# A Fourier front laid out anew: a root per tile in the tables, odd sums inside the eight-row products, four blocks at once

## Chip, cores and metric

The kernel runs on one core of a Trainium2 chip. The metric is the device time of one execution in microseconds (us). TensorE (PE in the profile, PEld for its weight loads), VectorE (DVE), ScalarE (ACT), GpSimd (POOL) and SyncE (SP) each work through a queue of their own in order and wait for each other on semaphores.

## The reference

```python
def fourier_mix(h, w_out):
    hg = h.astype(jnp.float32).reshape(B, S, N_FGROUPS, F_GROUP)      # 512 tokens, 8 groups of 128 features
    f = jnp.fft.fft2(hg, axes=(1, 3), norm="ortho").real
    return f.reshape(B, S, D_MODEL) @ w_out                           # 1024 x 1024

for i in range(2):
    if i == 0:
        x = x + fourier_mix(rms_norm(x, fourier_norm[0]), fourier_w_out[0])
    else:
        x = x + gqa_attention(rms_norm(x, attn_norm[0]), ...)
    x = x + sq_relu_mlp(rms_norm(x, mlp_norm[i]), mlp_w_up[i], mlp_w_down[i])
return rms_norm(x, final_norm)
```

It is done for two sequences of 512 tokens (`x_prompt`, `x_sample`), in float32. The change touches the Fourier layer alone, with which the kernel begins.

## The kernel before

**Numbers.** Most products are float32 accuracy out of three products of rounded parts (`mm3`: high x high, high x low, low x high). `split` makes the parts: ScalarE casts the high half, VectorE subtracts it for the low half. The first sequence's transform runs instead on unrounded float32 operands (`exact_*`), one product of which is two records in the trace.

**Front of a sequence.** The transform of real data is folded. Four tiles `xa[q, t]` of 128 tokens by 1024 features come in; `Front(q, c)` takes tiles 2c and 2c+1: `squares` (ScalarE, sums of squares), `gain` (VectorE, times the norm's gain), `plus` and `minus` (VectorE, sum and difference of the two feature halves; `plus_there` does the sum by an accumulating DMA issued on POOL), `chain` (the six small steps of 1/sqrt), then scaling by the root, and for c = 1 `combine`, which joins the two tiles. `ny` holds a few columns of the difference that need products of their own, with 40 columns of weights (`exact_nyq`, `seq_nyq`). The second sequence's parts are also split (`split_even`, `split_odd`, `split_hi`, `split_lo`).

**Transform.** `transform(q)` multiplies along the tokens for four feature blocks j: cosine into a PSUM tile `ps`, sine into another, over the parts k; then along the features (`feat_stage`: the u and v products, a correction by `feat_nyq` from `an`, and a product that picks odd features' sums into `en`), and splits u and v. Blocks 0 to 2 go together, block 3 after the first feature stage.

**Output weights.** `Fold(j)` loads two halves of the output weights; `minus` makes their difference on VectorE (odd weights) and starts an accumulating DMA on POOL for their sum (even weights). `odd`, `even_hi` and `even_lo` split them. The first sequence then has eight odd products (`odd_outs`, all at once) and eight even ones (`even_outs`, one after the other, in `even(fo)`); `odd_put` and `even_put` take them out of PSUM. An even output has 13 products: three for each of four blocks, and one with the extra rows of `FoldNyq`.

**Order and buffers.** Within `tc.manual_schedule` each engine's queue is in the order of the code, so where a step stands in the code is where it waits. PSUM has eight tiles, `ps()`, handed out in turn. The eight odd outputs hold all of them; even output fo takes the one that `odd_put(fo)` has emptied, and the second transform takes, for its first product and its three pairs of blocks, those that `even_put` 0 to 6 have emptied. `even_put` is a VectorE addition of 510 columns (L726) and a ScalarE copy of two columns (L727) behind it:

```python
nc.vector.tensor_add(both[:, :, 1:], o[:, 1:256].unsqueeze(1).broadcast_to([P, 2, 255]), both[:, :, 1:])
nc.scalar.copy(x[:, 0:257:256], o[:, 0:257:256])
```

The four tables of the second transform (`table(k)`: `dcos`, `dsin`, `dalt`, `dfeat`) and the additions of the input (`add_input`) are DMAs issued on POOL, in the same queue as the memset of `ny` in `combine`. At the start `idle` puts filler products on TensorE until the first data is there.

Of the kernel before, what the change touches and what calls it, by code (L numbers as in the profile page):

```python
# [44 lines left out]
def trunk_kernel(ctx, tc, x_in, xt_in, y_out, tables, rope, gfour, gcol, grow, gfin,  # L45
# [296 lines left out]
    def begin():  # L342
# [5 lines left out]
        for t in range(2, 4):  # L348
            load_x(0, t)
        exact_table(5)  # L350
        exact_table(6)
# [39 lines left out]
    def eights(x):  # L391
        return x[:, 0:512:64].unsqueeze(1).broadcast_to([P, 5, 8])

    class Front:


        def __init__(self, q, c):
            self.q, self.c = q, c
            self.ss, self.r = small(2), small(2)
            self.steps = rsqrt_steps(self.r[:, :2], self.ss[:, :2], 2, 1.0 / D)  # L400
            self.xg, self.p, self.m = [None] * 2, [None] * 2, [None] * 2

        def squares(self, i):
            sumsq(xa[self.q, 2 * self.c + i], self.ss[:, i : i + 1])

# [30 lines left out]
        def scale_both(self, i):  # L436
            if i == 0:
                self.n = sm.tile([P, 2, 5, 8], F32, tag="ny", name=nm("ny"), bufs=2, padded_shape=[P, 2, 8, 8])
            for out, x in ((self.p[i], self.p[i]), (self.n[:, i], eights(self.m[i])), (self.m[i], self.m[i])):
                nc.scalar.activation(out, x, AF.Copy, scale=self.r[:, i : i + 1])  # L440
            parts.append((self.p[i], self.m[i], self.n[:, i]))

        def combine(self):
            (p1, p2), (m1, m2), r, w = self.p, self.m, self.r, 8
            stt = nc.vector.scalar_tensor_tensor
            if self.q == 0:
                n = sm.tile([P, 5, 8], F32, tag="ny", name=nm("ny"), bufs=2, padded_shape=[P, 16, 8])
                stt(n, eights(m2), r[:, 1:2], eights(m1), ALU.mult, ALU.add)
# [60 lines left out]
    def exact_nyq(k, o):  # L509
        nc.tensor.matmul(o[0:40, :258], parts[k][2].rearrange("p a b -> p (a b)"), cosX[k], start=k == 0, stop=k == 2)  # L510
# [26 lines left out]
    def feat_nyq(u, j, first):  # L537
        nyt = nyqs[0][:, j * P : (j + 1) * P]
        nc.tensor.matmul(u[:, :258], nyt, an, start=first, stop=not first)
        return u  # L540

    def feat_stage(q, j, a, b, an, en, u=None):
        if q == 0:
            nc.tensor.matmul(u[:, :258], ftX[:, :P], a, start=False, stop=True)
        else:
            u = ps()
            mm3(u[:, :258], ft(0)[:, 0:P], ft(1)[:, 0:P], a[:, 0], a[:, 1], True, False)
            feat_nyq(u, j, False)
        v = ps()
        pick = slice(6 - 2 * j, 78 - 2 * j)  # L550
        if q == 0:
            nc.tensor.matmul(v[:, :256], ftX[:, P:], b, start=True, stop=True)
            nc.tensor.matmul(en[0:72, :258], pickX[:, pick], a, start=j == 0, stop=j == 3)
        else:
            mm3(v[:, :256], ft(0)[:, P:], ft(1)[:, P:], b[:, 0], b[:, 1], True, True)
            ent = tabs[2][:, 516:594][:, pick]
            nc.tensor.matmul(en[0:72, :258], ent, a[:, 0], start=j == 0, stop=False)
            nc.tensor.matmul(en[0:72, :258], ent, a[:, 1], start=False, stop=j == 3)
# [4 lines left out]

    def nyq_out(q, en):
        t = slot([P, 258], F32R)[0:72]
        nc.scalar.copy(t, en[0:72, :258])
        nc.vector.tensor_sub(t[64:72], en[64:72, :258], f32(t[64:72]))
        un[q] = t
# [4 lines left out]
    def idle(o, n):  # L573

        for _ in range(n):
            nc.tensor.matmul(o[:, :256], filler, filler.unsqueeze(1).broadcast_to([P, 2, P]), start=True, stop=True)  # L576

    def transform(q, mid=lambda: None, hook=lambda at, j: None):
        on, ov = ps(), [(ps(), ps()) for _ in range(3)]
        if q == 0:  # L580
            for k in range(2):
                for j in range(3):
                    exact_even(k, j, ov[j][0])
                exact_nyq(k, on)
                for j in range(3):
                    exact_odd(k, j, ov[j][1])
            mid()
            exact_nyq(2, on)
        else:
            seq_nyq(q, 0, on)  # L590
            for j in range(3):
                seq_part(q, j, 0, *ov[j])
            mid()
            seq_nyq(q, 1, on)
        en = ps()
        nc.scalar.copy(an[0:40], on[0:40, :258])
        nc.vector.tensor_sub(an[32:40], on[32:40, :258], f32(an[32:40]))
        ab = []
        for j in range(3):
            if q == 0:  # L600
                exact_odd(2, j, ov[j][1])
                exact_even(2, j, ov[j][0])
            else:
                seq_part(q, j, 1, *ov[j])
            ab.append(seq_evac(q, *ov[j]))
            hook("seq", j)
        us = [None] * 4
        if q == 0:
            us[0] = feat_nyq(ps(), 0, True)
        feat_stage(q, 0, *ab[0], an, en, us[0])  # L610
        hook("feat", 0)
        o3 = ps(), ps()
        if q == 0:
            for k in range(3):
                exact_even(k, 3, o3[0])
            for k in range(3):
                exact_odd(k, 3, o3[1])
        else:
            for c in range(2):
                seq_part(q, 3, c, *o3)  # L620
# [79 lines left out]
    def even_outs(q, fos):  # L700
        return outs(q, fos, we, 0, 258, (wn.w, un[q]))
# [1419 lines left out]
```

## Time and profile before

| | us |
|---|---|
| three runs | 1671.53, 1672.46, 1674.67 |
| profiled execution, its own time | 1673.12 |
| its span, first to last instruction | 1671.3 |
| TensorE busy | 1661.9 (99%) |
| VectorE busy | 1267.0 (76%) |
| ScalarE busy | 872.1 (52%) |
| POOL busy | 394.3 (24%) |

Times in the trace count from the first instruction. A row of the timeline has start, length, engine, line, operation, what it writes from what it reads, and a count where equal ones are merged; in square brackets is the engine's idle time before it and who ended it. A window's row has, for each engine, busy time and number of instructions. Line numbers are those of the kernel before.

### The profile page before, as it was taken

The page shows a single profiled execution, that of the slowest core. Times are in us where ns is not written, and L with a number is a line of the kernel's source. Part 1 is how long each engine was busy: PE and PEld are TensorE (multiplying, and loading weights), DVE is VectorE, ACT ScalarE, POOL GpSimd, SP SyncE. Part 2 cuts the span into 40 slices and gives each one's busy share as a digit, 9 for nine tenths or more (in the row PEclk, how much of TensorE's full clock was granted, in tenths as well). Part 3 has the DMA queues.
Part 4 walks back from the last instruction along what each step waited for, and adds up shares of the span by engine and source line. Part 5 has one row for each costly group of instructions (what it writes and reads, how often), then busy time and mean ns, then how long its engine had stood idle before and what let it go on. Part 6 is the DMA issues. An engine that isn't in the chain of part 4 may idle for free.

```text
span 1671.3 us, 22288 instructions
## 1 busy us (share of the span) xinstructions
PE 1661.9 (99%) x7843; PEld 1387.8 (83%) x7843; DVE 1267.0 (76%) x1851; ACT 872.1 (52%) x1540; POOL 394.3 (24%) x364
## 2 busy tenths in 40 slices
PE   9999999999999999999999999999999999999998
PEld 8988887888888888888888888888888888888887
DVE  8879776557886869869888877777855487878875
ACT  7766444446342435447688855554454552433334
POOL 3321444221000001325444303004422220000002
PEclk9999999999999999999999999999999999999999
DMA  9843554449775757425501156334544696757532
GB/s 306 257 158 118 204 195 172 151 170 373 250 228 165 248 170 236 168 77 200 166 1 39 64 176 223 117 120 167 211 145 166 221 375 194 233 158 236 178 104 101
DMA packets 122192, 302.48 MB, mean 181 GB/s; under 512 B 12344, under 2 KB 13496, under 8 KB 122080
## 3 DMA queue, kind: packets, MB, share of 16 engines
q1 hardware_dynamic: 98720, 253.53, 43.9%
q0 software_dynamic: 8960, 21.05, 6.0%
q10 hardware_dynamic: 14400, 26.48, 4.2%
q8 instruction: 61, 1.00, 0.2%
q14 instruction: 51, 0.42, 0.1%
HBM read 217.59 MB, written 82.38 MB: 179 GB/s over the span
## 4 chain that ended last, share of the span: by engine, by line
PE 97%; DVE 1%; DMA 0%; ACT 0%; issue 0%; POOL 0%; DVEq 0%; POOLq 0%; ACTq 0%
PE ps L940 74%; PE ps L83 6%; PE ps L81 6%; PE ps L82 6%; PE ps L1535 2%; PE ps L576 0%; PE ps L1514 0%; DMA raw<-w_up 0%; PE ps L191 0%; PE ps L507 0%; PE ps L504 0%; DVE w L87 0%; DVE raw L990 0%; PE ps L199 0%; DVE raw L989 0%
## 5 line engine op out<-in xcount | busy, mean ns | idle before, releaser
L940 PE MATMUL ps<-u,w 128*128 128x512 f32 x4944 | 1130.9, 389 | 1.2 <-DVE t L1018 1.2
L940 PEld LDWEIGHTS ps<-u,w 128*128 128x128 f32 x4944 | 926.6, 188 | 195.9 <-ACT u L973 1.7
L86 ACT CAST w<-raw 128x1024 fp32r<-128x1024 f32 (+1 forms) x216 | 213.7, 994 | 311.5 <-PE ps L940 234.3
L87 DVE TENSOR_TENSOR w<-raw,w 128x1024 fp32r<-128x1024 f32 (+1 forms) x216 | 252.0, 1170 | 75.7 <-ACT w L86 75.4
L86 ACT CAST u<-u 128x1024 fp32r<-128x1024 f32 x144 | 145.0, 1047 | 85.1 <-PE ps L940 36.4
L87 DVE TENSOR_TENSOR u<-u,u 128x1024 fp32r<-128x1024 f32 x144 | 174.3, 1239 | 17.3 <-ACT u L86 16.0
L940 PE MATMUL ps<-u,u 128*128 128x512 f32 x600 | 143.3, 389 | 0.0
L1150 DVE TENSOR_TENSOR u<-ps,u 128x512 f32<-128x512 f32 x160 | 109.9, 688 | 39.8 <-PE ps L940 37.3
L1177 POOL DMA_DIRECT2D raw<-w_sum x32 | 27.7, 865 | 468.2 <-DMA raw<-w_sum 170.8
L1058 POOL TENSOR_TENSOR u<-u 128x512 f32<-128x512 f32 x28 | 37.0, 1321 | 425.9 <-ACT u L955 425.9
L940 PEld LDWEIGHTS ps<-u,u 128*128 128x128 f32 x600 | 112.5, 188 | 24.1 <-ACT u L973 0.4
L81 PE MATMUL ps<-u,u 128*128 128x512 f32 (+2 forms) x340 | 128.7, 380 | 0.0
L83 PE MATMUL ps<-u,u 128*128 128x512 f32 (+2 forms) x340 | 123.7, 365 | 0.0
L82 PE MATMUL ps<-u,u 128*128 128x512 f32 (+2 forms) x340 | 123.6, 365 | 0.0
L182 POOL TENSOR_TENSOR t<-t,t 128x512 f32<-128x512 f32 (+1 forms) x54 | 79.2, 1470 | 187.0 <-ACT t L178 186.1
L954 ACT ACTIVATE t<-t 128x512 f32<-128x512 f32 x64 | 40.5, 632 | 109.2 <-DVE t L1027 95.7
L83 PEld LDWEIGHTS ps<-u,u 128*128 128x128 f32 x340 | 64.2, 189 | 10.5 <-DVE u L87 0.3
L87 DVE TENSOR_TENSOR u<-ps,u 128x512 fp32r<-128x512 f32 (+3 forms) x112 | 68.2, 636 | 5.6 <-ACT u L86 5.0
L82 PEld LDWEIGHTS ps<-u,u 128*128 128x128 f32 x340 | 64.4, 189 | 8.5 <-DVE u L87 0.3
L81 PEld LDWEIGHTS ps<-u,u 128*128 128x128 f32 x340 | 64.4, 189 | 7.8
L1014 DVE TENSOR_TENSOR t<-ps,u 128x512 f32<-128x512 f32 x32 | 22.0, 689 | 59.5 <-PE ps L940 55.8
L86 ACT CAST u<-ps 128x512 fp32r<-128x512 f32 (+3 forms) x112 | 59.5, 557 | 7.7 <-PE ps L1535 6.1
(270 smaller groups left out, 2024.6 us busy)
## 6 DMA issues: line engine op xcount, KB each, us to landing
raw<-w_up SPq DMA_DIRECT2D x80, 512.0 KB, 4.6
u<-spill_t SPq DMA_DIRECT2D x60, 512.0 KB, 6.7
raw<-w_sum SPq DMA_DIRECT2D x56, 512.0 KB, 5.5
u<-spill_b SPq DMA_DIRECT2D x45, 512.0 KB, 6.3
spill_t<-u SPq DMA_DIRECT2D x84, 256.0 KB, 2.0
spill_b<-t ACTq DMA_DIRECT2D x60, 256.0 KB, 4.4
raw<-w_row SPq DMA_DIRECT2D x28, 512.0 KB, 5.0
park<-u SPq DMA_DIRECT2D x24, 512.0 KB, 4.6
```

What stands on the lines that cost most here:

```text
L81: nc.tensor.matmul(out, lh, rh, start=first, stop=False)
L82: nc.tensor.matmul(out, lh, rl, start=False, stop=False)
L83: nc.tensor.matmul(out, ll, rh, start=False, stop=last)
L86: hi = nc.scalar.copy(dst_hi, src)
L87: return hi, eng.tensor_sub(dst_lo, src, f32(dst_hi))
L182: nc.gpsimd.tensor_add(acc[q][:, :n], acc[q][:, :n], s[:, :n])
L940: nc.tensor.matmul(o, w[x][:, sl], h[k][y], start=first and k + i == 0, stop=k == n - 1 and i == 2, skip_group_check=not first)
L954: nc.scalar.activation(t, src, AF.Relu)
L1058: eng.tensor_sub(t[:, 0], b12, b11)
L1150: return nc.vector.tensor_add(x, o, x)
L1177: nc.gpsimd.dma_start(s[:, 1], w[:, 3], accum_op=ALU.add)
L1535: nc.tensor.transpose(pt[:, t * P : (t + 1) * P], probs[t][:, sc * P : (sc + 1) * P], ident)
```

## The change

What it does, in the order of the code:

- The loads: table 1 comes before the fourth tile; table 2 comes behind the first fold's halves; all folds and the second sequence's tiles are asked for earlier in the code.
- The first two tiles get a root each (`apart`), and the root goes into the tables (`table`), not into the tiles; the steps of each root stand between long instructions on VectorE. Filler at the start is 23 products, not 39.
- The odd features' sums are no longer picked by a product for each block. VectorE sums the odd columns of each part (`odd_sums`, `tensor_reduce`), ScalarE copies the sums next to the eight `ny` columns (`put_sums`), and the eight-row products take both, with 56 columns of weights. `put_low` makes the extra rows of the even outputs from their result.
- The first transform is `transform_exact`: four blocks at once in all eight PSUM tiles, nine filler products with zero weights behind the second part, the eight-row products behind the third part, and two feature products ahead of each split.
- `hook0` and what follows are reordered: the differences of folds 0 to 2 in one row on VectorE, all four `even_hi` in one row on ScalarE ahead of the first `odd_put`, the second sequence's `gain`, `minus` and `plus_there` further ahead, the tables on POOL behind even output 1, both `combine`s ahead of the last even outputs.

```diff
-            self.steps = rsqrt_steps(self.r[:, :2], self.ss[:, :2], 2, 1.0 / D)
+            if q == 0 and c == 0:
+                self.apart = [rsqrt_steps(self.r[:, i : i + 1], self.ss[:, i : i + 1], 1, 1.0 / D) for i in range(2)]
+            else:
+                self.steps = rsqrt_steps(self.r[:, :2], self.ss[:, :2], 2, 1.0 / D)
...
+        def table(self, i):
+            t = exact[i][:, :514]
+            nc.scalar.activation(t, t, AF.Copy, scale=self.r[:, i : i + 1])
...
+    def odd_sums(k):
+        s = small(8)
+        x = parts[k][0].rearrange("p (g d i) -> p g d i", g=8, i=2)[:, :, :, 1]
+        nc.vector.tensor_reduce(s, x, AX.X, ALU.add)
+        return s
+
+    def put_sums(k, s):
+        nc.scalar.copy(parts[k][2][:, :, 1:], s.unsqueeze(1).unsqueeze(1).broadcast_to([P, 2, 3, 8]))
...
-        nc.tensor.matmul(o[0:40, :258], parts[k][2].rearrange("p a b -> p (a b)"), cosX[k], start=k == 0, stop=k == 2)
+        nc.tensor.matmul(o[0:56, :258], parts[k][2].rearrange("p a b c -> p (a b c)")[:, :56], cosX[k], start=k == 0, stop=k == 2)
...
+    def put_low(on):
+        norm = 1.0 / math.sqrt(S * P)
+        low = slot([P, 258], F32R)[0:56]
+        nc.scalar.activation(low, on[0:56, :258], AF.Copy, scale=norm)
+        nc.vector.scalar_tensor_tensor(low[32:56], on[32:56, :258], norm, f32(low[32:56]), ALU.mult, ALU.subtract)
+        un[0] = low
...
+    def transform_exact(mid, hook):
+        ov = [(ps(), ps()) for _ in range(4)]
+        for k in range(2):
+            for j in range(4):
+                exact_even(k, j, ov[j][0])
+            for j in range(4):
+                exact_odd(k, j, ov[j][1])
+        idle(ov[3][1], 9, an[:, :P])
+        mid()
+        ab = []
+        for j in range(4):
+            exact_odd(2, j, ov[j][1])
+            exact_even(2, j, ov[j][0])
+            ab.append(seq_evac(0, *ov[j]))
+            hook("seq", j)
+        on = ps()
+        for k in range(3):
+            exact_nyq(k, on)
+        put_an(on)
+        put_low(on)
+        hook("an", 0)
+        o = [feat_exact(*ab[j]) for j in range(2)]
+        for j in range(4):
+            feat_nyq(o[j][0], j)
+            feat_split(0, j, *o[j])
+            hook("feat", j)
+            if 0 < j < 3:
+                o.append(feat_exact(*ab[j + 1]))
...
-    idle(ps(), 39)
+    idle(ps(), 23)
...
+        g0.chain(0, 1)
+        g0.gain(0)
+        g0.chain(2, 3)
+        g0.minus(0)
+        g0.plus_there(0)
+        for j in range(4):
+            fold[j].even_hi()
...
+        odd_put(0, 0, o[0])
...
         even(0)
+        g1.gain(1)
         g1.minus(1)
         g1.plus_there(1)
-        g1.squares(1)
+        for k in range(4):
+            table(k)
         even(1)
+        g0.combine()
+        g1.chain(0, 1)
+        g1.chain(2, 3)
         even(2)
...
-        even(6)
         g1.combine()
         g1.split_hi()
+        even(5)
+        g1.split_lo()
+        even(6)
         even(7)
-        g1.split_lo()
```

The pieces of the queues that the prediction speaks of follow. In them, names like `u_` and `t_` are SBUF tiles, `s_` and `n_` small ones, `ps_` PSUM tiles; numbers differ between the two builds.

VectorE before, from the second sequence's first tile to the four low halves of the even weights (L659; `raw` and the `u_315` tile are the accumulated weights):

```order
L423 TENSOR_TENSOR t_431<-u_429 128x512
L410 TENSOR_TENSOR u_436<-u_321,u_99 128x1024
L423 TENSOR_TENSOR t_438<-u_436 128x512
L141 TENSOR_SCALAR s_259<-s_257 128x2
L143 RECIPROCAL s_260<-s_261 128x2
L144 TENSOR_TENSOR s_262<-s_260 128x2
L145 SCALAR_TENSOR_TENSOR s_262<-s_262,s_259 128x2
L146 SCALAR_TENSOR_TENSOR s_258<-s_262,s_260 128x2
L659 TENSOR_TENSOR w_551<-raw_249,w_551 128x1024
L659 TENSOR_TENSOR w_553<-raw_253,w_553 128x1024
L659 TENSOR_TENSOR w_564<-raw_311,w_564 128x1024
L659 TENSOR_TENSOR w_569<-u_315,w_569 128x1024
```

The same place on VectorE after (L700 are the low halves, L429 `gain`, L442 `minus`):

```order
L141 TENSOR_SCALAR s_160<-s_158 128x2
L429 TENSOR_TENSOR u_545<-u_238,u_99 128x1024
L143 RECIPROCAL s_161<-s_162 128x2
L442 TENSOR_TENSOR t_548<-u_545 128x512
L144 TENSOR_TENSOR s_163<-s_161 128x2
L700 TENSOR_TENSOR w_551<-raw_220,w_551 128x1024
L145 SCALAR_TENSOR_TENSOR s_163<-s_163,s_160 128x2
L700 TENSOR_TENSOR w_553<-raw_226,w_553 128x1024
L146 SCALAR_TENSOR_TENSOR s_159<-s_163,s_161 128x2
L429 TENSOR_TENSOR u_566<-u_240,u_99 128x1024
L700 TENSOR_TENSOR w_555<-raw_230,w_555 128x1024
L700 TENSOR_TENSOR w_557<-u_234,w_557 128x1024
```

The root's steps lie between long instructions now, the second `gain` stands between the second and the third low half, and its `minus` has gone behind the fourth.

VectorE before, at the last even outputs (L726 is `even_put`, L463 to L465 and L87 the second half's `combine`, L479 its low halves):

```order
L726 TENSOR_TENSOR u_443<-ps_697,u_443 128x2x255
L726 TENSOR_TENSOR u_443<-ps_714,u_443 128x2x255
L726 TENSOR_TENSOR u_444<-ps_732,u_444 128x2x255
L463 SCALAR_TENSOR_TENSOR n_153_750<-t_636,s_264,t_606 128x8
L464 SCALAR_TENSOR_TENSOR u_579<-u_612,s_264,u_579 128x512
L465 SCALAR_TENSOR_TENSOR t_636<-t_636,s_264,t_606 128x512
L87 TENSOR_TENSOR ny_748<-n_153_750,ny_748 128x2x8
L726 TENSOR_TENSOR u_444<-ps_760,u_444 128x2x255
L479 TENSOR_TENSOR u_756<-u_579,u_756 128x512
L479 TENSOR_TENSOR u_757<-t_636,u_757 128x512
```

The same place on VectorE after (L769 is `even_put`, L485 to L487 and L87 `combine`, L501 the low halves):

```order
L769 TENSOR_TENSOR u_437<-ps_685,u_437 128x2x255
L769 TENSOR_TENSOR u_438<-ps_703,u_438 128x2x255
L485 SCALAR_TENSOR_TENSOR n_157_721<-t_619,s_165,t_588 128x8
L486 SCALAR_TENSOR_TENSOR u_586<-u_617,s_165,u_586 128x512
L487 SCALAR_TENSOR_TENSOR t_619<-t_619,s_165,t_588 128x512
L87 TENSOR_TENSOR ny_719<-n_157_721,ny_719 128x2x8
L769 TENSOR_TENSOR u_438<-ps_731,u_438 128x2x255
L501 TENSOR_TENSOR u_727<-u_586,u_727 128x512
L501 TENSOR_TENSOR u_728<-t_619,u_728 128x512
L769 TENSOR_TENSOR u_439<-ps_750,u_439 128x2x255
L769 TENSOR_TENSOR u_439<-ps_766,u_439 128x2x255
```

Before, seven `even_put` (0 to 6) stand ahead of the second half's combine and one behind it; now five stand ahead, number 5 behind the combine, and 6 and 7 behind the low halves too.

POOL before, from the second sequence's first root to the first `add_input` (L419 `plus_there`, L430 a masked root for `combine`, L454 the memset of `ny`, L730 `add_input`):

```order
L430 TENSOR_TENSOR s_559<-s_258,mask 128x1
L454 MEMSET ny_585 128x128
L329 DMA u_594<-dcos 128x774
L329 DMA u_596<-dsin 128x1024
L329 DMA u_598<-dalt 128x594
L329 DMA u_600<-dfeat 128x512
L419 DMA u_579<-u_579 128x512
L419 DMA u_612<-u_612 128x512
L730 DMA u_441<-xt 128x1024
```

The same place on POOL after (L438, L449, L476 and L773 are the same steps in that order):

```order
L449 TENSOR_TENSOR s_564<-s_159,mask 128x1
L438 DMA u_566<-u_566 128x512
L438 DMA u_586<-u_586 128x512
L438 DMA u_617<-u_617 128x512
L329 DMA u_622<-dcos 128x774
L329 DMA u_624<-dsin 128x1024
L329 DMA u_626<-dalt 128x594
L329 DMA u_628<-dfeat 128x512
L773 DMA u_436<-xt 128x1024
L476 MEMSET ny_647 128x128
```

The memset of the first `ny`, which ScalarE's cast and VectorE's low half of it wait for, has gone behind all four tables and the first `add_input`, and the tables behind the last two `plus_there`.

More of the change, by code (lines that the diff above doesn't have):

```diff
@@ L741, in trunk_kernel @@
[L741 to L750 removed]
+        g0, g1 = [Front(1, c) for c in range(2)]
+        idle(ps(), 23)
+        f0.squares(0)
+        f0.gain(0, 0, halves_gr[0])
+        f0.root(0, 0, 2)
+        nc.scalar.copy(gr[:, :512], halves_gr[0])
@@ L751, in trunk_kernel @@
+        f0.gain(0, 1, halves_gr[1])
+        nc.scalar.copy(gr[:, 512:], halves_gr[1])
+        f0.root(0, 2, 6)
+        f0.table(0)
+        f0.plus(0)
+        f0.minus(0)
+        f0.squares(1)
+        wn.load()
+        fold = [Fold(0)]
+        exact_table(6)
+        fold += [Fold(j) for j in range(1, 4)]
+        for t in range(NT):
+            load_x(1, t)
+        nc.sync.dma_start(gc, gcol)
+        f0.gain(1)
+        f0.root(1, 0, 3)
         f1.squares(0)
-        f0.scale_both(0)
```

296 lines of the change are left out of this document (133 added, 163 removed).

## The prediction

> **What bounds the kernel now.** I read the page first, then the stages of its first 60 us, then the instructions of each engine there in order of time.
>
> ```profile
> PE 1661.9 (99%) x7843; PEld 1387.8 (83%) x7843; DVE 1267.0 (76%) x1851; ACT 872.1 (52%) x1540; POOL 394.3 (24%) x364
> PE 97%; DVE 1%; DMA 0%; ACT 0%; issue 0%; POOL 0%; DVEq 0%; POOLq 0%; ACTq 0%
> ```
>
> TensorE is the chain that ends last. Behind the Fourier part the change moves nothing, so whatever TensorE gains or loses up to the start of the second sequence's transform goes through to the end. The stages of the front (columns: time, PE, PEld, DVE, ACT, POOL busy, granted clock, DMA share, GB/s):
>
> ```profile
> 10.00:20.00 10.00, 10.00 (x48) 7.11 (x47) 9.79 (x18) 6.71 (x15) 3.71 (x4) 1.00 1.03 409
> 20.00:30.00 10.00, 10.00 (x51) 8.45 (x51) 9.94 (x15) 7.89 (x20) 4.29 (x6) 1.00 1.06 324
> 30.00:40.00 10.00, 10.00 (x86) 10.00 (x85) 9.23 (x15) 8.32 (x13) 4.76 (x7) 1.00 1.06 204
> 40.00:50.00 10.00, 10.00 (x86) 10.00 (x85) 9.42 (x16) 8.85 (x26) 2.42 (x5) 1.00 0.66 181
> 50.00:60.00 10.00, 10.00 (x86) 9.98 (x86) 8.78 (x23) 6.50 (x21) 4.67 (x7) 1.00 0.90 161
> ```
>
> TensorE is full, and VectorE nearly as full: 9.79, 9.94, 9.23, 9.42 and 8.78 of 10 us. There are two bounds side by side here, and a front that is shorter on TensorE alone meets VectorE at once. TensorE's marks (start, length; two records for each float32 product):
>
> ```profile
> 17.86 0.63 PE L510 MATMUL ps<-u,ny 128*40 128x258 f32 x2
> 18.42 0.70 PE L507 MATMUL ps<-u,t 128*128 128x256 f32 x2
> 22.55 1.47 PE L504 MATMUL ps<-u,t 128*128 128x258 f32 x6
> 23.86 1.46 PE L507 MATMUL ps<-u,t 128*128 128x256 f32 x6
> 29.24 0.47 PE L81 MATMUL ps<-u,u 128*128 128x256 f32 x1
> 40.93 0.28 PE L81 MATMUL ps<-u,w 128*128 128x258 f32 x1
> 42.26 0.28 PE L83 MATMUL ps<-u,w 128*128 128x258 f32 x1
> 53.42 0.28 PE L81 MATMUL ps<-u,ny 128*40 128x258 f32 x1
> ```
>
> Six records take 23.86 - 22.55 = 1.31, so a float32 product takes 0.434. Odd output products begin at 29.24, even ones at 40.93 (the fourth fold's low half is first read at 42.26), the second transform at 53.42. From 29 us on TensorE takes one product of 256 columns per 0.12 us (86 in 10 us).
>
> **The change on TensorE up to the odd products.** The filler products:
>
> ```profile
> 1.17 2.93 PE L576 MATMUL ps<-u 128*128 128x256 f32 x12 [1.17 <-DVE mask L369]
> 5.40:7.40 2.00, 1.94 (x9) 2.00 (x10) 1.00 1.01 406
> 7.50:10.90 3.40, 3.40 (x31) 3.40 (x30) 1.00 1.02 403
> ```
>
> The first ten weight loads take 0.20 us each, the later ones 3.40/30 = 0.113, and the last one ends at 10.9. Sixteen fewer end about 1.9 us sooner, near 9.0. Whether table 0 is scaled by then matters little, for the front's end doesn't follow: the third tile pair is VectorE's.
>
> ```profile
> 15.38 0.16 DVE L145 SCALAR_TENSOR_TENSOR s<-s,s 128x2 f32<-128x2 f32 x1
> 15.58 0.16 DVE L146 SCALAR_TENSOR_TENSOR s<-s,s 128x2 f32<-128x2 f32 x1
> 15.65 0.69 DVE L423 TENSOR_TENSOR t<-u 128x512 f32<-128x512 f32 x1
> 17.87 0.74 DVE L450 SCALAR_TENSOR_TENSOR t<-t,s,t 128x512 f32<-128x512 f32 x1
> ```
>
> A root step that the next one waits for costs 0.20, one with an independent instruction behind it 0.07. Ten steps become fifteen, but two thirds of them now stand in front of something independent: 5 x 0.20 + 10 x 0.07 = 1.7, as much as ten cost before. So the combined pair is ready at 17.9 and 18.6, as before, and TensorE, which has done its 16 products at 9.0 + 16 x 0.434 = 16.0 and its nine fillers at 17.1, waits there.
>
> From the pair on, before: 29.24 - 18.42 = 10.8. After: eight products 3.5, three eight-row products, eight feature products 3.5, four short ones 0.5. An eight-row product in the middle of others took 18.42 - 17.86 = 0.56, and some 0.3 of drain ahead of it; three in a row I put at 0.3 + 3 x 0.56 = 2.0 (1.5 if only the first and last pay). Sum 9.5, odd products at 27.6: 1.6 gained (1.2 to 2.1). Some 0.7 of it goes in the odd products' first round, whose seventh and eighth bank wait for the fourth block's splits on VectorE.
>
> **VectorE from 18.5 to the even products.** Now the low halves, `even_lo`, end here:
>
> ```profile
> 31.04 1.23 DVE L87 TENSOR_TENSOR u<-u,u 128x1024 fp32r<-128x1024 f32 x1 [0.56 <-issue]
> 36.64 3.50 DVE L659 TENSOR_TENSOR w<-raw,w 128x1024 fp32r<-128x1024 f32 x3
> 40.28 1.23 DVE L659 TENSOR_TENSOR w<-u,w 128x1024 fp32r<-128x1024 f32 x1 [0.15 <-ACT w L655]
> 18.59 0.37 ACT L596 CAST u<-ps 40x258 fp32r<-40x258 f32 x1 [0.97 <-PE ps L510]
> L1525 DVE TENSOR_REDUCE s<-ps 128x1 f32<-128x512 f32 x64 | 43.7, 684 | 8.9 <-PE ps L83 6.8 <-PE ps L1535 1.9
> ```
>
> The queue ends at 41.5 and TensorE needs it at 42.26: 0.75 of slack. Added: three sums of 256 elements, between 0.16 (the least step) and 0.68 (the row's 512 from PSUM), taken as 0.37 each, 1.1. Added too: VectorE is free at 18.5 + 1.1 + 3 x 1.14 = 23.0, but its next instruction waits for the eight-row products (end 23.6, with ScalarE's 0.37 and a hop 24.1) and then once more for ScalarE's second copy: 1.5 (0.8 to 1.9). Gone: a `minus` moved behind (0.6), root steps between long ones (0.4), the old wait of 0.56 and 0.15 before the last. Two small waits on ScalarE add 0.4. Net +0.9 and the fourth low half at 42.4: that product starts at 42.45 against 42.26. **The gain of 1.6 is gone here and has become a loss of 0.2**; ScalarE's `odd_put`, now behind all four `even_hi`, lets the first even product start at about 40.3 and costs nothing more, if the last accumulated weight lands near 38.6.
>
> **From there to the second transform.** Its seven banks are those that even products 0 to 6 held, in turn, and each comes free with VectorE's and ScalarE's two `even_put` reads. The rows of now:
>
> ```profile
> 43.51 0.75 DVE L465 SCALAR_TENSOR_TENSOR t<-t,s,t 128x512 f32<-128x512 f32 x1
> 45.96 1.22 DVE L410 TENSOR_TENSOR u<-u,u 128x1024 f32<-128x1024 f32 x1
> 48.42 0.68 DVE L423 TENSOR_TENSOR t<-u 128x512 f32<-128x512 f32 x1
> 51.54 1.88 DVE L726 TENSOR_TENSOR u<-ps,u 128x510 f32<-128x510 f32 x3
> 55.16 0.68 DVE L726 TENSOR_TENSOR u<-ps,u 128x510 f32<-128x510 f32 x1
> 56.35 0.69 DVE L479 TENSOR_TENSOR u<-t,u 128x512 fp32r<-128x512 f32 x1
> 45.10 0.72 ACT L489 ACTIVATE t<-u,s 1x512 f32<-1x512 f32 x1
> 38.01 1.70 POOL L329 DMA_DIRECT2D u<-dcos  x1
> 40.81 0.53 POOL L329 DMA_DIRECT2D u<-dfeat  x1
> 49.78 0.89 POOL L419 DMA_DIRECT2D u<-u  x1 [3.54 <-PE ps L697]
> 50.42 2.04 POOL L730 DMA_DIRECT2D u<-xt  x2
> 53.49 0.86 POOL L730 DMA_DIRECT2D u<-xt  x1 [1.03 <-ACT u L727]
> 54.03 0.54 POOL L454 MEMSET ny<- 128x128 f32 x1
> ```
>
> Now puts 0 to 6 are over at 53.42, and only put 7 stands behind the second half's combine. After, VectorE does from 42.4: minus 0.6, gain 1.2, minus 0.6, put 0.6, gain 1.2, minus 0.6 (to 47.3), put 0.6, then the first half's combine (two small, 0.7, 0.75) to 49.5. There it waits for the low half of `ny`, whose high half on ScalarE waits for POOL's memset, and that now stands behind six issues: the last `plus_there` (released at 47.3), four tables and the first `add_input`. Issues follow each other at 0.65 (49.78 to 50.42) and 0.54 (53.49 to 54.03); the four tables took 38.01 to 41.34, 0.83 each, with waits among them. I take 0.65: 47.3 + 5 x 0.65 + 0.54 + 0.54 = 51.7, `ny` at 52.0 (51.4 with 0.54, 53.2 with 0.83). **VectorE stands 2.5 us, with six puts queued behind it.** Then: put 2 to 52.9; behind it ScalarE casts the even half (512 columns, 0.6 to 0.7 by the 45.10 row), so that low half ends at 54.4; ScalarE's one-row repair (0.72) and cast of the odd half, low half at 55.6; the root's last step 55.7; puts 3 and 4 to 56.9, while ScalarE scales the second half's two sums until 57.2; its combine, 2 x 0.7, to 58.6; put 5 to 59.3, two low halves to 60.5, put 6 to 61.1, ScalarE's read to 61.35.
>
> TensorE begins the transform at 42.45 + 0.24 + 7 x 1.56 = 53.6, waits 0.9 for the split halves and puts 3 and 4 until 57.7, for put 5 until 59.6, for put 6 until 61.4. It is past its seventh bank at 61.7; before, 53.42 + 21 x 0.12 = 55.9. **Sum: +5.8.** On VectorE nothing of that can be hidden. What the second half needs later is ready by then.
>
> By the Trainium skill, GPSIMD Engine Reference (Specifications), POOL's SBUF interfaces are shared with VectorE, with contention when a VectorE instruction has two SBUF inputs. The row of 1.70, an issue beside VectorE's low halves with two SBUF inputs, would be such a case; if five of them took that, `ny` would be 5 x 1.05 = 5.2 later and the sum +11. The rows of 0.86 and 0.89, beside VectorE's work too, and the next table's end 41.34 speak against it, so 0.65 stays.
>
> The profiled execution took 1673.12 with a span of 1671.3, and the three runs a median of 1672.46; its rows serve for both. 1672.46 + 5.8 = 1678.3.
>
> **The rivals.**
> (a) *The gain stays.* TensorE's 1.6 us hold if put 6 is done by 54 instead of 61, that is if VectorE loses neither the 1.5 for the eight-row products nor the 2.5 at `ny` and makes 3 us elsewhere. Time 1670.9. For it: TensorE is the page's bound. Against: VectorE's 9.4 of 10. Even with no wait at all TensorE could be at the odd products at 9.0 + 6.9 + 1.1 + 9.5 = 26.5, only 2.7 us sooner. It decides where VectorE's queue reaches put 6 before 55.8. Chance 0.08.
> (b) *POOL does not hold VectorE.* Issues are quicker or their order matters less; VectorE goes on at 49.5. Everything behind is 2.5 to 2.8 us earlier, put 6 at 58.5, since it stands behind both combines anyway: +3.0, 1675.5. Chance 0.18.
> (c) *The waits slow TensorE's clock.* It would work 2.5 us in eight. The opening's fillers were slow from 1.17 to 7.4; if TensorE fell back to 0.20 for as long, 6.2 us would do the work of 3.5: 2.7 more, 1681.0. The Trainium skill, TensorE: Matmul & The Clock Gate (What's actually happening), has the clock fall after an idle window of about 3.4 us, and no wait here is that long; the same page (A second HAM failure mode) has short waits for PSUM banks do it. By the first rule (c) doesn't happen; before's trace has no such waits to show either. Chance 0.12.
>
> **How the numbers follow.** The worked case has 0.56, by itself 1676.3 to 1680.0 (eight-row products -0.7, sums -0.6 to +0.9, issues -0.6 to +1.2, not all at once); 0.06 is left for what I haven't seen, half of it on either side of the faster bound. Eight in ten lie between 1674.0, below (b), and 1681.6, above (c). 0.2% is 3.3 us, about what measurement tells from none: 1675.8 and up counts as slower. That holds (c), the worked case and a third of (b), 0.74; (a), most of (b) and some of the rest are the same, 0.23; for faster TensorE would have to gain over 3.3, more than its front can give: 0.03.
>
> **What would show it.** Right: odd products near 27.6; VectorE idle near 23 to 24 behind the eight-row products and near 49.5 to 52 behind ScalarE's `ny`; TensorE idle in the second transform at each of its last four banks, released by ScalarE's two-column `even_put` copy; the first product of its second half near 61.7. Wrong: no gaps on TensorE there, or the three eight-row products ended before 22.5, or `ny`'s memset before 50.

## The result: 10 us slower, nearly twice what was forecast, and the profile after

The changed kernel takes 1683.64 us (median of six runs, 1683.03 to 1684.87); six runs of the kernel before beside them have 1673.59. The ratio is 1.0062, 95% interval 1.0049 to 1.0075. The forecast was 1678.3 and at most 1681.6: the sign was right, the size not. Medians here and below are of fast runs; two slow ones, 2917.5 us of the second version below and 1838.0 us of the kernel before beside the ninth, are left out.

The page of the changed kernel, busy time and chain that ended last:

```profile
span 1681.5 us, 22269 instructions
PE 1667.6 (99%) x7828; PEld 1388.7 (83%) x7828; DVE 1265.3 (75%) x1858; ACT 870.8 (52%) x1542; POOL 395.7 (24%) x364
PE 94%; DVE 3%; DMA 1%; ACT 1%; issue 1%; POOL 0%; DVEq 0%; POOLq 0%; ACTq 0%
```

The span grew by 10.2 us, and VectorE's share of the chain from 1% to 3%. Stages of the front (columns as before):

```profile
40.00:50.00 10.00, 9.50 (x64) 8.16 (x63) 8.97 (x13) 7.35 (x23) 7.82 (x7) 1.00 0.42 72
50.00:60.00 10.00, 8.46 (x57) 7.09 (x55) 6.09 (x17) 4.91 (x13) 2.82 (x6) 1.00 0.94 219
```

From 40 to 50 us TensorE gets 64 products done where it did 86, though it reads as nearly full and its clock is 1.00. From 50 to 60 VectorE is down to 6.09; 3.57 of what is missing is one wait. TensorE's marks:

```profile
21.71 1.51 PE L532 MATMUL ps<-u,ny 128*56 128x258 f32 x6
23.15 0.70 PE L582 MATMUL ps<-u,u 128*128 128x256 f32 x2
...
27.20 0.28 PE L81 MATMUL ps<-u,u 128*128 128x256 f32 x1
...
41.97 0.38 PE L83 MATMUL ps<-u,w 128*128 128x258 f32 x1 [0.50 <-DVE w L700]
...
56.27 0.31 PE L81 MATMUL ps<-u,ny 128*40 128x258 f32 x1
...
62.45 0.42 PE L521 MATMUL ps<-u,ny 128*40 128x258 f32 x1
...
124.89 0.62 PE L199 MATMUL ps<-ident,s 128*128 128x128 f32 x4 [0.22 <-DVE s L146]
```

Against the kernel before: odd products 2.04 sooner (29.24), fourth low half read 0.29 sooner (42.26), second transform begun 2.85 later (53.42). Its second half, the 22nd product of that transform, is at 62.45, and the last row stands behind the Fourier layers of both sequences. Their rows of before are these:

```profile
55.92 0.28 PE L499 MATMUL ps<-u,ny 128*40 128x258 f32 x1
...
113.90 0.62 PE L199 MATMUL ps<-ident,s 128*128 128x128 f32 x4 [0.23 <-DVE s L146]
```

So TensorE is 6.53 late at the second half and 10.99 late behind the Fourier layers. I call these two places the second half and the layer's end below.

**The first surprise** is in the weight loads of the even outputs (grouped by line and shape; the last figure is idle time before them), from 42 to 56.4 us and then in the second sequence:

```profile
L81 PEld LDWEIGHTS ps<-u,w 128*128 128x128 f32 x28 | 5.3, 190 | 0.9
...
L740 PEld LDWEIGHTS ps<-u,u 56*128 56x128 f32 x8 | 1.5, 183 | 1.1
...
L740 PEld LDWEIGHTS ps<-u,u 48*128 48x128 f32 x8 | 1.5, 183 | 1.1
```

TensorE stands before each of the 16 extra-row products (1.1/8 = 0.14 us) and again behind it. The change cut that product from 72 rows to 56, and to 48 in the second sequence. In time order:

```profile
43.91 0.19 PEld L83 LDWEIGHTS ps<-u,w 128*128 128x128 f32 x1
44.23 0.18 PEld L740 LDWEIGHTS ps<-u,u 56*128 56x128 f32 x1
44.55 0.19 PEld L81 LDWEIGHTS ps<-u,w 128*128 128x128 f32 x1
...
46.50 0.19 PEld L81 LDWEIGHTS ps<-u,w 128*128 128x128 f32 x1
```

The steps into and out of it take 0.32 each where 0.12 is usual, and the even output takes 46.50 - 44.55 = 1.95 instead of 1.56: 0.39 more, 3.1 us per sequence.

**The hold-up** of VectorE behind POOL came as forecast, and longer (rows of POOL, ScalarE, VectorE):

```profile
51.80 0.53 POOL L476 MEMSET ny<- 128x128 f32 x1
...
52.37 0.22 ACT L86 CAST ny<-n 128x32 fp32r<-128x32 f32 x1 [4.74 <-POOL ny L476]
...
52.62 0.19 DVE L87 TENSOR_TENSOR ny<-n,ny 128x32 fp32r<-128x32 f32 x1 [3.57 <-ACT ny L86]
```

**The last banks**: TensorE's weight loads in the second transform, with the idle time ahead of them:

```profile
60.12 0.19 PEld L81 LDWEIGHTS ps<-u,u 128*128 128x128 f32 x1 [1.86 <-ACT u L770]
...
61.91 0.19 PEld L81 LDWEIGHTS ps<-u,u 128*128 128x128 f32 x1 [1.38 <-ACT u L770]
```

Both waits were forecast, for 59.6 and 61.4, with ScalarE's two-column copy as the releaser. The stages behind them:

```profile
62.00:64.00 2.00, 2.00 (x11) 1.86 (x12) 0.26 (x1) 0.39 (x2) 0.89 (x1) 0.56 1.03 152
64.00:66.00 2.00, 2.00 (x12) 2.00 (x12) 0.96 (x3) 1.03 (x4) 0.00 (x0) 0.58 1.13 205
66.00:68.00 2.00, 2.00 (x19) 2.00 (x18) 1.27 (x4) 2.00 (x7) 0.41 (x1) 1.00 1.02 207
```

The clock is 0.56 to 0.58 for some 4 us: 23 products where 38 are usual, 15 x 0.105 = 1.6 us.

### The profile page after: what moved, and what is told of

The parts are those of the page before. It is cut to its first block, busy times and chain, and to the rows that moved or that the text cites. A ratio compares the mean times of both kernels' runs of the same rounds, so it can differ in the third digit from the quotient of the medians.

```text
span 1681.5 us, 22269 instructions
## 1 busy us (share of the span) xinstructions
PE 1667.6 (99%) x7828; PEld 1388.7 (83%) x7828; DVE 1265.3 (75%) x1858; ACT 870.8 (52%) x1542; POOL 395.7 (24%) x364
## 4 chain that ended last, share of the span: by engine, by line
PE 94%; DVE 3%; DMA 1%; ACT 1%; issue 1%; POOL 0%; DVEq 0%; POOLq 0%; ACTq 0%
PE ps L1003 73%; PE ps L81 6%; PE ps L83 6%; PE ps L82 6%; PE ps L1598 2%; DVE u L429 0%; PE ps L1577 0%; PE ps L191 0%; DMA u<-w_four 0%; ACT u L86 0%; DMA raw<-w_sum 0%; DMA u<-spill_t 0%; DVE t L442 0%; DMA u<-x 0%; DVE u L87 0%
## 5 line engine op out<-in xcount | busy, mean ns | idle before, releaser
L87 DVE TENSOR_TENSOR w<-raw,w 128x1024 fp32r<-128x1024 f32 (+1 forms) x216 | 251.2, 1167 | 75.7 <-ACT w L86 75.4
L86 ACT CAST u<-u 128x1024 fp32r<-128x1024 f32 (+1 forms) x140 | 140.7, 1047 | 86.4 <-PE ps L1003 38.9
L87 DVE TENSOR_TENSOR u<-u,u 128x1024 fp32r<-128x1024 f32 (+1 forms) x140 | 168.7, 1232 | 18.3 <-ACT u L86 17.8
L87 DVE TENSOR_TENSOR u<-ps,u 128x512 fp32r<-128x512 f32 (+3 forms) x112 | 68.1, 633 | 6.2 <-ACT u L86 5.7
L1077 DVE TENSOR_TENSOR t<-ps,u 128x512 f32<-128x512 f32 x32 | 22.0, 686 | 60.3 <-PE ps L1003 56.7
```

The lines of the kernel that those rows point to most:

```text
L86: hi = nc.scalar.copy(dst_hi, src)
L87: return hi, eng.tensor_sub(dst_lo, src, f32(dst_hi))
```

## The experiments

The theories: (R) the extra product costs 0.39 us where it has 64 rows or fewer; (H) POOL's queue holds VectorE, and so the banks; (C) the bank waits lower the clock; and whether VectorE's queue as a whole takes the front's gain. The last column is the median less that of the kernel before, run beside it in the same series.

| kernel | second half | layer's end | median | less before |
|---|---|---|---|---|
| before | 55.92 | 113.90 | | |
| changed | 62.45 | 124.89 | 1683.64 | +10.05 |
| 1, 72 rows | 62.68 | 122.01 | 1679.65 | +7.25 |
| 2, clears early | 58.67 | 119.67 | 1677.73 | +5.33 |
| 3, before with 64 rows | 58.88 | 119.86 | 1677.83 | +5.43 |
| 4, products in the waits | 62.54 | 123.53 | 1681.86 | +9.46 |
| 5, both of 1 and 2 | 58.98 | 118.31 | 1676.03 | +3.61 |
| 6, and puts ahead | 56.64 | 115.36 | 1674.14 | +1.72 |
| 7, and VectorE's stands | 56.51 | 115.89 | 1673.91 | +1.49 |
| 8, and one gain late | 56.96 | 116.74 | 1674.54 | +2.01 |
| 9, and tables early | 55.87 | 115.34 | 1673.58 | +1.39 |
| 10, two tables early | 54.80 | 114.81 | 1673.17 | +0.49 |

Differences of medians are to be read with care. The kernel before varies by some 3 us from run to run; its six runs beside the changed kernel have a median of 1673.59, in the other series it is 1672.2 to 1672.7. So a difference between the changed kernel and a version is about 1.2 larger by the medians themselves than by the last column, and differences of 1 us between versions are not clear of the noise. The marks, from one profiled execution each, carry the argument.

**1. The rows back.**

```diff
-        low = slot([P, 258], F32R)[0:56]
-        nc.scalar.activation(low, on[0:56, :258], AF.Copy, scale=norm)
+        low = slot([P, 258], F32R)[0:72]
+        nc.gpsimd.memset(f32(low[64:72]), 0.0)
+        nc.scalar.activation(low[0:64], on[0:64, :258], AF.Copy, scale=norm)
...
-        return outs(q, fos, we, 0, 258, (wn.w[: 48 if q else 56], un[q]))
+        return outs(q, fos, we, 0, 258, (wn.w, un[q]))
```

> The changed kernel with its extra product, the last one of each even output, back to 72 rows (the added rows hold zeros in the weights; the eight-row products take 64 columns and the second sequence's pick 72, so that the rows exist). Rows theory: with 56 or 48 rows TensorE pauses 0.14 us before and 0.13 after that product, and an even output takes 1.95 us instead of 1.56. Then the pauses go, the second transform begins near 53.2 instead of 56.3, but still waits for the same banks until 61.9, so the first eight outputs bring nothing and the second sequence's eight bring 8 x 0.39 = 3.1: 3.1 us faster than the changed kernel (2.6 to 3.6), near 1680.5. If TensorE and not VectorE set the end of the first eight: 6.2 faster. If the pauses come from something else than the count of rows: no change, and the gaps stay.

The layer's end came 2.88 sooner, the median 2.8 by the last column (4.0 by the medians themselves): the second sequence's 3.1 and nothing for the first eight, as expected. The extra product's weight loads in the second sequence (grouped):

```profile
L741 PEld LDWEIGHTS ps<-u,u 72*128 72x128 f32 x8 | 1.5, 191 | 0.0
```

No idle time is left. TensorE where it then stands, in order of time:

```profile
60.07 0.58 PE L81 MATMUL ps<-u,u 128*128 128x258 f32 x1 [1.66 <-ACT u L771]
...
61.87 0.58 PE L81 MATMUL ps<-u,u 128*128 128x256 f32 x1 [0.79 <-ACT u L771]
```

The waits at the banks end where they did (60.12 and 61.91). TensorE, at the transform earlier, has more waits there, and its granted clock is down sooner (0.72 from 58 to 60 us, 0.50 to 64), which fits the second half's 0.23 of delay.

**2. The clears early.** The memset of `ny` is taken out of `combine` and stands in a step of its own, `clear`:

```diff
         o = odd_outs(0, range(KC))
+        g0.clear()
+        g1.clear()
         g0.chain(0, 1)
```

> The changed kernel with the two clears of the second sequence's eight-row tiles put on the Pool queue right behind the odd products, ahead of the accumulating transfers and the four tables. Hold-up theory: VectorE's stand of 3.57 us at 49 to 52.6 goes, puts 2 to 6 come 3.4 us earlier, TensorE's waits for banks (0.14 + 1.86 + 1.38) nearly go, and with them the low granted clock of 62 to 66 us, which costs 1.5: 4.9 us faster than the changed kernel, near 1678.7. If the low clock comes from something else than those waits: 3.4 faster. If VectorE isn't what the banks wait for: no change.

The layer's end came 5.22 sooner, 3.78 of it at the second half and 1.44 behind it, the median 4.7 by the last column. In order of time, the two clears and VectorE's low half of `ny`, which no longer waits:

```profile
33.73 0.68 POOL L467 MEMSET ny<- 128x128 f32 x2
...
48.82 0.18 DVE L87 TENSOR_TENSOR ny<-n,ny 128x32 fp32r<-128x32 f32 x1
```

The stage in which the changed kernel had a clock of 0.56:

```profile
62.00:64.00 2.00, 2.00 (x19) 2.00 (x18) 1.38 (x5) 2.00 (x7) 1.44 (x2) 1.00 1.08 213
```

H holds, and it carries the clock with it. TensorE has no wait in that transform here. It begins it at 56.13, late by its own pauses: in the first sequence the pauses and the hold-up lie side by side, and the longer one counts.

**3. The kernel before with 64 rows.**

```diff
-        return outs(q, fos, we, 0, 258, (wn.w, un[q]))
+        return outs(q, fos, we, 0, 258, (wn.w[:64], un[q][:64]))
```

> The kernel before with its extra product cut from 72 rows to 64 (the last eight, the low part of that operand, are left out of the computation), and nothing else. Rows theory: two pauses of 0.13 to 0.14 us and a slower product at each of 16 even outputs, 0.39 us each, 6.2 us, of which 1.6 go into a later wait of TensorE (1.57 at 260 us) that is there anyway: 4.6 us slower than the kernel before (4 to 6.2), near 1677. If the count of rows isn't the cause: no change within 0.5.

+5.43, ratio 1.0034 (1.0022 to 1.0046), and at the layer's end +5.96, half of it (2.96) by the second half. The row count alone costs this in a kernel that has nothing else of the change (the eight rows of low parts are left out of the computation). Its extra product's weight loads of the first sequence (grouped, idle time last):

```profile
L697 PEld LDWEIGHTS ps<-u,u 64*128 64x128 f32 x8 | 1.5, 183 | 1.1
```

So 64 rows pause like 56 and 48, and 72 do not. What lies between 64 and 72 wasn't tried. By the Trainium skill, TensorEngine Tiling (Array Packing), Key Properties, changing the tiling mode drains TensorE, and its Performance Considerations name row tiling for contractions of 64 rows and fewer. A pause on both sides, 0.14 us before and 0.13 after, and the step between 64 and 72 rows fit that; that the mode changes here no trace shows. The same section has column tiling for 64 weight columns and fewer; there the trace of the changed kernel shows no pause behind such a product with these rounded operands (TensorE in order of time):

```profile
56.54 0.28 PE L83 MATMUL ps<-u,ny 128*40 128x258 f32 x1
56.66 0.28 PE L81 MATMUL ps<-u,u 128*128 128x258 f32 x1
```

From 40 columns to 128 is the usual 0.12.

**4. Products in the waits.**

```diff
             seq_part(q, j, 0, *ov[j])
+            for _ in range((14, 10, 0)[j]):
+                nc.tensor.matmul(ov[0][1][:, :256], zero[:, 0:1].broadcast_to([P, P]), sinT()[:, 0, :256], start=False, stop=False)
```

> The changed kernel with 14 and 10 products with zero weights put into an open bank where TensorE waits 1.86 and 1.38 us for the second transform's last banks, so that it works through those waits. Clock theory: the granted clock of 0.56 to 0.58 from 62 to 66 us comes from the short waits before it, so it stays at 1.00 and 14 products fewer are late: 1.5 us faster than the changed kernel. If the low clock has another cause: it stays, and the time is the same or up to 0.3 worse.

TensorE passes the last bank no sooner:

```profile
62.08 0.39 PE L81 MATMUL ps<-u,u 128*128 128x256 f32 x1 [0.59 <-ACT u L774]
```

But the stage behind it runs at full clock:

```profile
62.00:64.00 2.00, 1.92 (x16) 1.91 (x17) 0.71 (x2) 0.64 (x4) 0.89 (x1) 1.00 1.06 164
```

The layer's end moved by 1.36, the median's distance from the kernel before by 0.6, where the interval (1.0037 to 1.0067) overlaps the changed kernel's: that comparison alone doesn't show it, though the runs themselves lie apart (1681.13 to 1681.88 against 1683.03 to 1684.87, in another series). The clock theory rests on the rows: with products in the waits the clock isn't lowered. The Trainium skill, TensorE: Matmul & The Clock Gate, has under What's actually happening a clock that falls after an idle window of about 3.4 us and, under A second HAM failure mode, one that falls with short waits for PSUM banks; the longest single wait here was 1.86, so the second fits better.

**5. Both.** The edits of 1 and 2 together.

> The changed kernel with both edits: extra product on 72 rows, and the two clears early on the Pool queue. VectorE's end of put 6 (58.1 with the early clears alone) doesn't depend on TensorE, so TensorE, now ready for the second transform at 53.1, waits again for puts 5 and 6 (56.1 and 58.1) and is past its seventh bank near 58.2. Against the early clears alone only the second sequence's eight outputs gain: 3.1 us, 1674.7; if those two waits of 1.5 us each lower the granted clock again, up to 1.5 of it is lost: 1676.2. Rival, the two gains simply add: 1683.6 - 4.0 - 5.9 = 1673.8.

By the marks the gains don't add: 124.89 - 2.88 - 5.22 would put the layer's end at 116.79, and it is at 118.31. The median is near the 1676.2 that was expected for the case that the waits lower the clock again. TensorE, sooner at the second transform, waits again:

```profile
58.38 0.38 PE L81 MATMUL ps<-u,u 128*128 128x256 f32 x1 [1.18 <-ACT u L774]
```

And it loses clock again, in the stage behind that:

```profile
60.00:62.00 2.00, 2.00 (x12) 2.00 (x11) 0.64 (x2) 0.75 (x2) 0.23 (x1) 0.50 1.04 207
```

**6. Puts ahead.**

```diff
+        even(5)
+        even(6)
         g1.combine()
         g1.split_hi()
-        even(5)
         g1.split_lo()
-        even(6)
         even(7)
```

> As the run with both edits, and even outputs 5 and 6 are put ahead of the second half's combine (as in the kernel before), not behind it and its low halves. If VectorE's order is what holds the banks: put 6 near 55.0, no bank wait over 0.5 us, but the second half's eight-row tile is then ready only near 56.7, where TensorE waits about 1 us at its 22nd product: 1673.2 (1672.5 to 1674). If TensorE's bound is elsewhere: as the run with both edits.

The second half starts at 56.64 (56.7 expected), but its delay of 0.72 is a stand at 54.75, not the eight-row tile: the number was hit by luck. The time is 0.1 above the range. TensorE begins the second transform at 53.42, to the hundredth where the kernel before does. The stand is at the first product that reads the second table; the profile puts it down to a copy (rows of the weight load, the table's issue on POOL, and its transfer, whose last figure is the time from issue to landing):

```profile
54.75 0.19 PEld L81 LDWEIGHTS ps<-u,u 128*128 128x128 f32 x1 [0.67 <-ACT u L774]
...
48.84 0.75 POOL L329 DMA_DIRECT2D u<-dsin  x1
...
u<-dsin POOLq DMA_DIRECT2D x1, 512.0 KB, 5.8
```

48.84 + 5.8 = 54.64, 0.11 ahead of the start, so the table's landing is the likelier releaser; at the same product of run 8, below, the profile names that transfer. In run 5 that product stands too, 0.45.

**7. VectorE's stands filled.** The first fold's odd low half ahead of `put_an`, the first half's casts ahead of put 2, `odd_put` 0 and 1 ahead of the fourth `even_hi`. (`hook("nyq", 0)` calls `fold[0].odd_lo()`; `first_hi` holds both casts, and the low halves stay behind put 2.)

```diff
+        hook("nyq", 0)
         put_an(on)
...
         g0.combine()
+        g0.first_hi()
```

> As the run before it, with VectorE's three stands filled: the first fold's odd low half ahead of the eight-row products' result (stands of 0.91 and 0.45), the first half's casts on ScalarE ahead of put 2 (0.68 and 0.51), and two odd puts ahead of ScalarE's cast of the fourth fold (0.8 on TensorE at the first even output). If VectorE alone keeps the front's gain from TensorE: put 6 near 53, the second half's tile near 55, the fourth low half a microsecond sooner, no wait at the banks: 1671.6 (1670.8 to 1672.6), 0.8 faster than the kernel before at most 1.5. Rival, the 1.0 us go into the next wait (landing of accumulated weights or the second half's loads): 1672.5 to 1673.5.

My theory fell: 1673.9. The low half of the fourth fold came no sooner (TensorE reads it at 42.16), because the first stand, 0.91 in run 6, came back as two other waits for ScalarE, and the second, 0.45, stayed:

```profile
25.02 0.42 DVE L623 SCALAR_TENSOR_TENSOR u<-ps,u 24x258 fp32r<-24x258 f32 x1 [0.45 <-ACT u L622]
25.90 1.42 DVE L87 TENSOR_TENSOR u<-ps,u 128x257 fp32r<-128x257 f32 x4 [0.46 <-ACT u L86]
27.95 0.76 DVE L87 TENSOR_TENSOR u<-ps,u 128x257 fp32r<-128x257 f32 x2 [0.63 <-ACT u L86]
```

**8. One gain late.**

```diff
-        g0.gain(1)
         fold[2].even_lo()
...
         fold[3].even_lo()
+        g0.gain(1)
```

> As the last run, and one instruction of VectorE that the second sequence needs (a gain of 1.13 us, issued ahead of the third fold's even low half) goes behind the fourth fold's. VectorE's total stays. Theory, VectorE's queue as a whole takes the front's gain: the fourth low half is read by TensorE near 41.2 instead of 42.16 and the second transform begins near 52.5 instead of 53.37, but the puts and the second half come no sooner, so TensorE's wait at the transform's banks grows from 0.47 to about 1.4 and the second half's eight-row product starts at 56.4 as before: 1673.9 within 0.5 of the last run. Rival, only the place of the fourth low half holds the gain: everything from 42 us on comes 0.9 sooner, 1673.0, or less by what the wait near 260 us takes (1.57 in the kernel before).

The low half is read at 41.16, a microsecond sooner; the second half starts at 56.96 all the same, and the time is no better: 1674.54, 0.6 above the last run where within 0.5 was expected. But the first wait stands ahead of the transform, not in it (POOL's issue of the first table, and TensorE):

```profile
48.56 0.81 POOL L329 DMA_DIRECT2D u<-dcos  x1
...
53.79 0.11 PEld L81 LDWEIGHTS ps<-u,ny 128*40 128x40 f32 x1 [1.16 <-ACT u L785]
...
55.09 0.35 PE L81 MATMUL ps<-u,u 128*128 128x256 f32 x1 [0.38 <-DMA u<-dsin]
```

The transfer itself (the last figure is the time from issue to landing):

```profile
u<-dcos POOLq DMA_DIRECT2D x1, 387.0 KB, 5.1
```

48.56 + 5.1 = 53.7: the first product would be standing until the first table lands, though the profile puts it down to a copy. Run 9 tests that. The change had moved the tables from 38.01 on POOL's queue to 48.20.

**9. Tables early.**

```diff
         g0.plus_there(1)
+        for k in range(4):
+            table(k)
...
-        for k in range(4):
-            table(k)
```

> As the last run, and the four tables of the second transform are issued on the Pool queue four steps sooner, ahead of the second half's two accumulating transfers (in the kernel before they were issued near 38 us and landed by 45.5; in the changed one near 48, landing at 53.3 to 56.3). In the last run TensorE was ready for the second transform at 52.7, began at 53.79, 0.1 behind the first table's landing (53.69), and stood once more 0.56 until the second table's (54.96). Tables theory: both waits go, the transform begins near 52.7, the second half's eight-row product starts near 55.8, where VectorE's and ScalarE's work on it ends, and all behind comes 1.0 sooner: 1673.5. Rival, puts and not tables hold the first bank (the profile names ScalarE's copy): the start stays at 53.8 and the time at 1674.5. In either case VectorE's queue keeps the time from falling below the kernel before by more than 0.5.

It was the tables: the transform begins at 52.53, without a wait ahead of it, and the layer's end comes 1.4 sooner. The time, 1673.58, is the one expected (1673.5), but its interval (0.9998 to 1.0016) overlaps run 8's (1.0002 to 1.0020). VectorE, in its own order, now waits for the transfer that the tables went past:

```profile
55.20 0.75 DVE L489 SCALAR_TENSOR_TENSOR u<-u,s,u 128x512 f32<-128x512 f32 x1 [0.89 <-DMA u<-u]
```

**10. Two tables early.** `range(2)` there, the other two behind the transfers.

> As the last run, but only the first two tables go ahead of the second half's accumulating transfers, the other two behind them as before. In the last run the second of those transfers landed at 55.10 and VectorE stood 0.89 us for it in the second half's combine, so that half's eight-row tile came 0.9 late again. If that wait goes: TensorE's second half from 55.6 without a stop, the first reduction of the second sequence near 70.1 instead of 70.98 (69.93 in the kernel before), the time 1672.7 (1672.2 to 1673.4), level with the kernel before. If the transfer waits for its slot's reader and not for the queue: landing near 55 still, and the time as the last run's, 1673.6.

The wait for the transfer is gone. TensorE's weight loads in the second sequence's first even output, in order of time:

```profile
66.17 0.19 PEld L81 LDWEIGHTS ps<-u,w 128*128 128x128 f32 x1 [0.25 <-ACT u L86]
66.69 0.19 PEld L82 LDWEIGHTS ps<-u,w 128*128 128x128 f32 x1 [0.34 <-DVE u L87]
```

The second half is at 54.80, 1.12 sooner than in the kernel before: here the front's gain is there at last. It is lost again by the layer's end (114.81, 0.91 late). Of these 2.03 us the weight loads show 1.32 in five short stands between 55 and 68 us, each put down to ScalarE or VectorE; at the two above TensorE has reached the operand before ScalarE's cast and VectorE's low half of it are done. The time, 1673.17, lies in the expected range and has a ratio of 1.0004 (0.9995 to 1.0013) to the kernel before: not to be told from none. No version beat the kernel before.

## Why the prediction was right and wrong

- **Front on TensorE: right.** 2.04 gained at the odd products against 1.6 (1.2 to 2.1). TensorE began on the combined pair at 17.82 and took 9.38 to the odd products, where 9.5 was put; in part that is luck, for the eight products ahead took 3.89 instead of 3.5, and the three eight-row products, put at 2.0, took 23.15 - 21.71 = 1.44. From the 18.42 of its own sum the 9.5 would have given 27.9, not 27.6.
- **The gain gone at the fourth low half: right**, with the residue's sign missed (0.3 ahead, not 0.2 behind). VectorE's three sums were put at 1.1 and its two stands at the eight-row products at 1.5; its rows have 1.07 and 0.90 + 0.45:

```profile
18.34 1.07 DVE L400 TENSOR_REDUCE s<-t 128x8 f32<-128x256 f32 x3
...
23.72 0.42 DVE L603 TENSOR_TENSOR u<-ps,u 8x258 fp32r<-8x258 f32 x1 [0.90 <-ACT u L602]
24.58 0.42 DVE L609 SCALAR_TENSOR_TENSOR u<-ps,u 24x258 fp32r<-24x258 f32 x1 [0.45 <-ACT u L608]
```

- **The step that failed: "Behind the Fourier part the change moves nothing, so whatever TensorE gains or loses up to the start of the second sequence's transform goes through to the end."** The second sequence's transform and its eight even outputs still belong to the Fourier part, but the sum stopped at that transform's 22nd product, where it had +5.8 and the changed kernel shows 6.53. From there to the layer's end it had no term, and there the changed kernel takes 62.44 us where the kernel before takes 57.98. With 72 rows (run 1) it is 59.33, so 3.1 are the extra products of the second sequence's eight even outputs; with products in the waits (run 4) it is 60.99, so 1.45 are the lowered clock. That the extra product went from 72 rows to 56 and 48 stood in the full diff, and no term was made of it. The same omission is in "TensorE begins the transform at 42.45 + 0.24 + 7 x 1.56 = 53.6": it kept 1.56 for an output that now takes 1.95, and the transform begins at 56.27. That cost nothing in the first sequence, where VectorE covered it (run 1: nothing gained there); so the last bank's 61.4, which came out as 61.91, says nothing for 53.6.
- **VectorE behind POOL: right in kind, small in size.** It was to stand 2.5 and stood 3.57, partly because it was there sooner, at 49.05 instead of 49.5; `ny` was ready at 52.62 instead of 52.0. Rival (b) fell with that stand; run 2 shows the price of the hold-up, 5.22 at the layer's end with the clock in it. The bound with POOL slowed to 1.70 an issue didn't come: these issues took 0.57 to 0.88.
- **The clock: a rival that was a term.** I gave (c) 0.12 as another way to go; it was no alternative but followed from the waits that the sum itself had. It cost 1.4 to 1.6, where 2.7 was put; that price came from the opening's fillers, whose own row has a granted clock of 1.00. Even the sum with (c), 1681.0, stays 2.6 below the 1683.64; the extra products' 3.1 are not in it.
- **The tables: a step moved past a queue, and not costed.** I counted their issues as the hold-up and not their landing. In the changed kernel other waits hid it; from run 5 on the second table's landing comes forward at one product (0.45 to 0.67), and in run 8 the first one's too.

The sum with the measured terms: 6.53 at the second half (the forecast's 5.8, `ny` 0.6 later, and 0.2 for the last three products at the lowered clock), 3.1 for the second sequence's extra products and 1.45 for the clock are 11.1, against 10.99 at the layer's end. Of that the profiled spans show 10.2 and the medians 10.05 (interval 8.2 to 12.6). One taker is a wait of TensorE for VectorE that the trace of the kernel before has and that of the changed one has not; how much it takes was not tried:

```profile
260.25 0.30 PEld L940 LDWEIGHTS ps<-u,w 128*128 128x128 f32 x2 [1.57 <-DVE t L1018]
```

## What to carry to other kernels

Cost a change of a product's shape at every place where that shape occurs, and follow the sum to the last of them: 16 products with fewer rows, at 0.39 us each, were missing from the sum, and half of them showed in the time. A gain on one engine is worth what the next full engine's queue leaves of it; here VectorE's queue, waits for ScalarE and the tables' landing kept the front's 2 us from the second half until run 10, and short stands behind it took them even there. Waits that a forecast puts on TensorE should carry their clock with them.

## What was not expected of the hardware

A product of 64, 56 or 48 rows between products of 128 rows costs TensorE 0.39 us more than one of 72 rows, and PE's busy time hides most of it: 9.50 of 10 us with 64 products where 86 took 10.00. Two waits of 1.86 and 1.38 us within 4 us lowered the granted clock to 0.56 for about 4 us; a wait of 1.16 with a shorter one behind it (run 8), and one of 0.67 (run 6), did not; what separates the two cases was not tried.
